# A hybrid decoder block on one core: another form of the routing, the first gather and the last expert block

## The chip, the core and the metric

The kernel runs on one core of one Trainium2 chip. The metric is the time of the program on the device in microseconds (us), the median of three runs: 1419.67 us (1419.36 to 1420.41). Engine names are those of the profile: PE is TensorE, PEld its weight loads, DVE is VectorE, ACT is ScalarE, POOL is GpSimd, SP is SyncE, which issues nearly all loads.

## What is computed

One decoder layer over 256 tokens of width 2048, all in float32. Cut to what matters:

```python
h = rms_norm(x, norm_mix_g);  proj = h @ w_in          # 2048 -> 7168 columns
o = concat([moba_attention(...), hgrn2(...)])          # 8 heads of attention, 8 of gated recurrence
x = x + o @ w_out
h2 = rms_norm(x, norm_ffn_g)
# routing: 4 groups, 4 experts in a group; the best group, then the best two experts in it
grp_w, grp_idx = top_k(softmax(h2 @ w_grp + b_grp), 1)
top_w, top_idx = top_k(softmax(expert logits of that group), 2)
top_w = top_w / sum(top_w) * grp_w
x = x + sum over the 16 experts: ((silu(h2 @ w_gate) * (h2 @ w_up)) * weight) @ w_down
return rms_norm(x, final_norm_g)
```

An expert has three weight matrices of 2048 x 1024 float32, 8 MB each. All 16 experts together are 403 MB, and each is read once.

## The kernel before

**First part** (to about 475 us): the projections, attention and recurrence, then `w_out` in two halves of the contraction (`proj_n`, L366, and the loop after L715). The weights come in 1 MB pieces through two raw halves `shared[8][:, 0]` and `[:, 1]` (`issue_raw`, L103), ACT and DVE split each into a high and a low part (`units`, L305), and PE multiplies. Background work stands in a queue of generators, `bgq`: after each unit `step(k)` (L234) lets it go on by k steps. In the second half of `w_out` the last two column blocks are 256 wide (blocks 3 and 4), and each block appends an `out_block` (L688): DVE adds the block to `X`, ACT takes its square sums into `ssq`, PE transposes it, DVE copies the transposes, PE multiplies them by the router's weights `wr` into `pl`.

**Routing** (L723 to L787): when the queue is empty, `pl` is copied and folded into the logits `plt` (L734 to L738), the root of the mean square is taken, Z is made (L746), and `first_max` (L750) finds the first maximum twice by maximum, comparison, multiplication by a falling count, maximum and comparison. `selb` marks the chosen experts of each token, five small products count ranks (`pr`), and `rk` holds the rank of each token in each expert. `keep_busy` (L729) puts products without use between these steps on PE. `weights_of_routes` (L797) makes the routing weights `comb`, in its last line it writes `cmaxi`, which at the very end decides whether an expert had more than 64 tokens (a branch not taken here).

**Experts** (from L932): each expert has room for 64 tokens (`CAP`). `gather_matrix(e)` makes a 256 x 64 matrix with one entry for each token taken; `gather` (L850) multiplies it with `X` in 512-wide products into one two-bank tile, with a copy by ACT of each bank; `turn` (L863) transposes the result into `xg` and multiplies by the norm's gain. `stream` (L903) runs over the four pieces of the gate (`ga`) and of up (`up`), 16 products of 512 columns for each piece, of which two run side by side in the two halves of the array. Then `hid` = silu(ga) * up, its transposes `hT`, and four pieces of the down matrix into `pd`. `scatter` (L892) adds the result to `acc` in the next expert, behind the first piece of its gate. The order on PE is that of the program (`mmo`, `transpose`); elsewhere a planner orders what is ready. For expert e + 1 the gather stands between `hid` and the down pieces of expert e.

**Loads.** A piece is 2 MB (`pieces`, L247). Twelve loads are issued before the experts (`early_loads`, L249): eight in the course of the first part (`ahead`, L303), the others when the queue is empty (L724). Piece 8 takes the whole of slot 8, that is both raw halves together. Piece 0 is loaded in halves, the second one into a slot that `w_out` uses until its end. Each piece that PE has used up lets `advance` (L822) put the next load on SP's queue, into the slot of an earlier piece: from piece 12 on the nine slots of `ring` in turn, so that piece n waits for the reading of piece n - 9 or n - 10. The loads are in order on SP's queue. In expert 0 the tile `rest`, which holds `hid`, takes the slot of piece 7, the last one of up (L951). `final_gain` (L922), 16 products and four copies, stands behind the third gate piece of expert 1.

**Last expert** (L985 to L1025): the down matrix comes by four column blocks in two halves each. Block b goes into half of one bank of `pd`, a two-bank tile, ACT copies it to `osl`; `spread(b)` (L989) multiplies it into `pz` behind the first half of block b + 1; DVE adds that to `acc`, ACT squares it with a sum into `fs`, POOL multiplies by the final gain (DVE in block 3). At the end the root of the mean square (`rstd`, L198), the scaling of `y` by DVE and ACT in two halves each, and four stores on SP's queue.

Of the kernel before, what the change touches and what calls it, by code (L numbers as in the profile page):

```python
# [19 lines left out]
P = 128  # L20
# [17 lines left out]
def hybrid_block_kernel(  # L38
# [149 lines left out]
    rev = cst.tile([P, 4], F32, name="rev")  # L188
    nc.gpsimd.iota(rev, pattern=[[-1, 4]], base=4, channel_multiplier=0,
                   allow_small_or_imprecise_dtypes=True)  # L190
# [51 lines left out]
    def drain():  # L242
        while bgq:
# [6 lines left out]
                   (8, 8), (9, 9), (10, 7), (0, 1, 1)]  # L250
    ring = [d[1] for d in early_loads if len(d) == 2 and d[0] != 7]
# [17 lines left out]
    def load():  # L269
# [5 lines left out]
        if len(at) == 2:  # L275
            hf, s = at
            wt = single(s, [P, 2048], name="wt")
# [88 lines left out]
    def proj_n(aTh, aTl, c0=0, c1=NC, w=512):  # L366
# [3 lines left out]
        while c < c1:  # L370
            for hi, lo in units():
# [8 lines left out]
                step(2 if c0 else 1)  # L380
# [306 lines left out]

    def out_block(b, col, w, pp, last):  # L688
# [10 lines left out]
        for j in range(0, k, 2):  # L699
            xT = xTs[xi[0] % 2]  # L700
            xi[0] += 1
            pt = psmall().rearrange("p (j t) -> p j t", j=2)
            for i in range(2):
                for n in range(NT):
                    nc.tensor.transpose(
                        pt[:, i, n * P:(n + 1) * P],
                        x2[:, n, bs].rearrange("p (q j) -> p j q", j=k)[:, j + i], ident)
            V.tensor_copy(xT, pt)
            yield
            for i in range(2):  # L710
                mm(pl[32 * i:32 * i + 32], wr[:, col // P + j + i], xT[:, i],
                   start=b == 0 and j == 0, stop=b == 4)
# [16 lines left out]
    def keep_busy(k, ps, lhs, rhs):  # L729
        for i in range(k):  # L730
            mm(ps[0:lhs.shape[1], 0:P], lhs, rhs, start=True, stop=True)

    keep_busy(8, busy, ident, x2[:, 1, D - P:])
    lt = dist1[0:64]  # L734
    V.tensor_copy(lt, pl)
    plt = psmall()[:, :40].rearrange("p (n e) -> p n e", n=NT)
    for n in range(NT):
        mm(plt[:, n], lt[:, n * P:(n + 1) * P], fold[0:64], start=True, stop=True)  # L738


    r2 = small8[:, 2:4]
    V.tensor_reduce(r2, ssq, AX.X, ALU.add)
    rstd(r2, r2, D)
    Z = cst.tile([P, 5, NT, 4], F32, name="Z")
    for n in range(NT):
        V.scalar_tensor_tensor(Z[:, :, n], plt[:, n].rearrange("p (g e) -> p g e", g=5),  # L746
# [3 lines left out]
    def first_max(dst, src, m, tmp, vm, k):  # L750

        V.tensor_reduce(m, src, AX.X, ALU.max)
        V.tensor_tensor(tmp, src, m.unsqueeze(2).to_broadcast([P, k, 4]), ALU.is_equal)
        V.tensor_tensor(tmp, tmp, rev.unsqueeze(1).to_broadcast([P, k, 4]), ALU.mult)
        V.tensor_reduce(vm, tmp, AX.X, ALU.max)
        V.tensor_tensor(dst, tmp, vm.unsqueeze(2).to_broadcast([P, k, 4]), ALU.is_equal)

    Zf = Z.rearrange("p g n e -> p (g n) e")
    ma = cst.tile([P, 10], F32, name="ma")
    mb = cst.tile([P, 8], F32, name="mb")  # L760
    vm = cst.tile([P, 10], F32, name="vm")
    tmp = cst.tile([P, 10, 4], F32, name="tmp")
    M1 = cst.tile([P, 10, 4], F32, name="M1")
    M2 = cst.tile([P, 8, 4], F32, name="M2")
    E2 = cst.tile([P, 8, 4], F32, name="E2")
    keep_busy(8, busy, Z.rearrange("p g n e -> p (g n e)"), ident)
    first_max(M1, Zf, ma, tmp, vm, 10)
    keep_busy(6, busy, M1.rearrange("p a e -> p (a e)"), ident)
    V.scalar_tensor_tensor(E2, M1[:, 0:8], -1e30, Zf[:, 0:8], ALU.mult, ALU.add)
    first_max(M2, E2, mb, tmp[:, 0:8], vm[:, 0:8], 8)  # L770
    V.tensor_tensor(M2, M2, M1[:, 0:8], ALU.add)
    gm = M1[:, 8:10].rearrange("p n g -> p g n").unsqueeze(3).to_broadcast([P, 4, NT, 4])
    selb = cst.tile([P, 4, NT, 4], BF16, name="selb")
    V.tensor_tensor(selb, M2.rearrange("p (g n) e -> p g n e", g=4), gm, ALU.mult)
    pr = psmall()[:, :48].rearrange("p (a g e) -> p a g e", a=3, g=4)
    mm(pr[:, 0], before, selb[:, :, 0], start=True, stop=True)
    mm(pr[:, 1], ones, selb[:, :, 0], start=True, stop=False)
    mm(pr[:, 1], before, selb[:, :, 1], start=False, stop=True)
# [353 lines left out]
```

## Time and profile before

| | us |
|---|---|
| median of 3 runs | 1419.67 |
| the profiled execution | 1415.9 |
| its span, first to last instruction | 1414.1 |
| PE busy | 1322.3 (94%) |
| DVE busy | 432.9 (31%) |
| ACT busy | 275.3 (19%) |
| POOL busy | 17.5 (1%) |
| DMA: mean over the span | 342 GB/s, 483.75 MB |

The profile shows one execution. A row of the timeline has start, duration, engine, line, operation, out<-in, and in brackets the idle time of the engine before it with what ended that. Rows of the same operation behind one another are merged (x8). A float32 product of PE has two records, a transpose one. "To landing" is the time from a load's issue to its arrival. Nearly all of the DMA's bytes are expert weights, so its share of busy time tells by stage whether the weights flow without a break.

### The profile page before, as it was taken

The numbers are of one execution on the slowest core, as the hardware profiler recorded it, in microseconds if no ns is written. First come the engines' busy times: TensorE is split into PE (matmuls) and PEld (weight loads), VectorE is DVE, ScalarE is ACT, GpSimd is POOL, SyncE is SP. The second block draws the span as 40 slices with busy tenths as digits, with TensorE's granted clock in tenths as the row PEclk, the third lists the DMA queues.
The fourth block names the chain that finished last, engine by engine and source line by source line (L and its number), as shares of the span: only waits on it lengthen the run. The fifth ranks groups of instructions, "written<-read, shape, count | busy, mean of one in ns | idle before, by whom it ended". The sixth has DMA issues, their size and how long they took to land.

```text
span 1414.1 us, 16501 instructions
## 1 busy us (share of the span) xinstructions
PE 1322.3 (94%) x7091; PEld 721.7 (51%) x7091; DVE 432.9 (31%) x647; ACT 275.3 (19%) x409; POOL 17.5 (1%) x47
## 2 busy tenths in 40 slices
PE   9999999999999999999999999889898998989885
PEld 8999998998887633333333323223232232322323
DVE  5555567567555411121121112111121111211012
ACT  5553542542543201000000000000000000000002
POOL 2000000000000000000000000000000000000002
PEclk9999999999999999999999999999999999999998
DMA  6655553455687599999999999999999999999995
GB/s 237 241 163 173 179 173 126 157 183 185 222 338 286 219 409 378 427 428 428 427 428 427 429 427 427 428 429 428 426 430 427 428 427 427 428 427 429 427 410 197
DMA packets 85726, 483.75 MB, mean 342 GB/s; under 512 B 16849, under 2 KB 19601, under 8 KB 60817
## 3 DMA queue, kind: packets, MB, share of 16 engines
q1 hardware_dynamic: 85520, 482.62, 84.6%
q8 instruction: 57, 0.93, 0.3%
q14 instruction: 21, 0.16, 0.0%
q10 hardware_dynamic: 128, 0.03, 0.0%
HBM read 480.54 MB, written 2.10 MB: 341 GB/s over the span
## 4 chain that ended last, share of the span: by engine, by line
PE 66%; DMA 29%; DVE 2%; ACT 2%; issue 1%; ACTq 0%; SPq 0%; DVEq 0%
DMA wt<-in_w_up_dram 25%; PE pd L831 12%; PE pp L340 12%; PE up L831 8%; PE ga L831 6%; PE pp L376 5%; PE pp L377 5%; PE pp L378 5%; PE pn L831 4%; DMA wt<-in_w_gate_dram 3%; PE pt L834 2%; PE pw L482 1%; PE psc L831 1%; DVE rest L967 1%; ACT xn L860 1%
## 5 line engine op out<-in xcount | busy, mean ns | idle before, releaser
L831 PE MATMUL up<-wt,xg 128*64 128x512 f32 x1024 | 231.2, 597 | 38.4 <-DMA wt<-in_w_up_dram 38.4
L831 PE MATMUL ga<-wt,xg 128*64 128x512 f32 x1024 | 226.8, 595 | 4.2 <-DMA wt<-in_w_gate_dram 4.2
L831 PE MATMUL pd<-wt,rest 128*64 128x512 f32 (+1 forms) x1088 | 224.7, 569 | 2.8 <-ACT rest L1016 2.0
L321 DVE TENSOR_TENSOR whl<-sh,whl 128x1024 fp32r<-128x1024 f32 (+1 forms) x145 | 175.5, 1216 | 121.9 <-ACT whl L319 116.8
L319 ACT ACTIVATE whl<-sh 128x1024 fp32r<-128x1024 f32 (+1 forms) x145 | 151.7, 1051 | 223.4 <-PE pp L378 106.0
L340 PE MATMUL pp<-hTh,whl 128*128 128x256 f32 x1024 | 190.4, 285 | 0.0
L831 PEld LDWEIGHTS up<-wt,xg 128*64 128x64 f32 x1024 | 69.4, 137 | 188.1 <-issue 120.3
L340 PEld LDWEIGHTS pp<-hTh,whl 128*128 128x128 f32 x1024 | 161.3, 192 | 0.2
L831 PEld LDWEIGHTS ga<-wt,xg 128*64 128x64 f32 x1024 | 72.9, 137 | 153.7 <-issue 149.8
L831 PEld LDWEIGHTS pd<-wt,rest 128*64 128x64 f32 x1088 | 76.2, 137 | 139.2 <-issue 128.9
L340 PE MATMUL pp<-hTl,whl 128*128 128x256 f32 x512 | 145.2, 284 | 1.1 <-DVE hTl L394 1.0
L901 DVE TENSOR_TENSOR rest<-rest,psc 128x1024 f32<-128x1024 f32 x28 | 34.2, 1221 | 254.4 <-PE psc L831 253.0
L340 PEld LDWEIGHTS pp<-hTl,whl 128*128 128x128 f32 x512 | 98.2, 192 | 1.9 <-DVE hTl L394 1.7
L887 DVE COPY pT<-pt 128x256 f32<-128x256 f32 x16 | 6.8, 424 | 292.5 <-PE pt L834 292.5
L376 PE MATMUL pp<-whl,hTh 128*128 128x512 f32 x192 | 77.5, 404 | 0.0
L860 ACT ACTIVATE xn<-pn 128x512 f32<-128x512 f32 x32 | 19.1, 597 | 295.6 <-PE pn L831 295.6
L378 PE MATMUL pp<-whl,hTl 128*128 128x512 f32 x192 | 75.3, 392 | 0.0
L377 PE MATMUL pp<-whl,hTh 128*128 128x512 f32 x192 | 74.9, 390 | 0.0
L831 PE MATMUL pn<-X,pg 128*64 128x512 f32 x256 | 61.2, 599 | 13.1 <-ACT xn L860 12.4
L831 PE MATMUL psc<-rest,pT 64*128 64x512 f32 x240 | 63.7, 628 | 7.0 <-DVE rest L901 7.0
L957 ACT ACTIVATE rest<-ga 128x512 f32<-128x512 f32 x16 | 9.6, 597 | 281.3 <-PE ga L831 253.6
L981 ACT ACTIVATE rest<-pd 128x1024 f32<-128x1024 f32 x15 | 15.4, 1025 | 234.3 <-PE pd L831 234.3
(273 smaller groups left out, 977.6 us busy)
## 6 DMA issues: line engine op xcount, KB each, us to landing
wt<-in_w_gate_dram SPq DMA_DIRECT2D x63, 2048.0 KB, 39.1
wt<-in_w_up_dram SPq DMA_DIRECT2D x60, 2048.0 KB, 34.9
wt<-in_w_down_dram SPq DMA_DIRECT2D x59, 2048.0 KB, 36.9
sh<-in_w_in_dram SPq DMA_DIRECT2D x55, 1024.0 KB, 5.1
sh<-in_w_out_dram SPq DMA_DIRECT2D x16, 1024.0 KB, 5.7
wt<-in_w_down_dram SPq DMA_DIRECT2D x8, 1024.0 KB, 14.7
wt<-in_w_up_dram SPq DMA_DIRECT2D x8, 1024.0 KB, 28.8
wt<-in_w_gate_dram SPq DMA_DIRECT2D x2, 1024.0 KB, 10.8
```

The source lines that it names most:

```text
L319: S.activation(t[:, 0, a:b], rw, AF.Copy)
L321: V.tensor_tensor(t[:, 1, a:b], rw, t[:, 0, a:b].bitcast(F32), ALU.subtract)
L340: r = mm(*a, **kw)
L376: mm(pp[:, n], ah, hi[:, k], start=c == c0, stop=False)
L377: mm(pp[:, n], ah, lo[:, k], start=False, stop=False)
L378: mm(pp[:, n], al, hi[:, k], start=False, stop=c == c1 - 1)
L482: mm(pa[:, 2 * h + n], k[:, h, ts], q[:, h, ts].rearrange("p (b z m) -> p b z m", z=2, m=m)[:, :, 1], start=True, stop=True)
L831: tc.keep_in_program_order(mm(*a, **k))
L834: tc.keep_in_program_order(nc.tensor.transpose(dst, src, ident))
L860: S.activation(xn[:, j], ps[:, j], AF.Copy)
L901: V.tensor_tensor(acc[n][:, bs], x2[:, n, bs] if e == 0 else acc[n][:, bs], ps.rearrange("p z f -> p (z f)"), ALU.add)
L981: S.activation(osb, pd, AF.Copy)
```

## The change

- **Loads.** Piece 8 is loaded in two halves of 1 MB straight into the raw halves of slot 8, each as soon as its own half is free.
- **Router products.** In the 256-wide blocks `step(4)` instead of `step(2)`. Block 3 ends the accumulation in `pl`, then copies it and folds it into `plt` at once, and takes the square sums of blocks 0 to 3 together. Block 4 is transposed by token halves, and its products go straight into `plt` with the transposes as the stationary side.
- **Choice of experts by counting.** Instead of two `first_max`, two comparisons of all pairs (160 elements), a choice between them by the mask `tri`, and a sum give each expert's rank; rank 0 is the best group, rank under 2 the two experts. `cmax` is taken from a copy that ACT makes, behind the gather matrix. `keep_busy` has 3, 6 and 3 products instead of 8, 8 and 6, and is kept in program order.
- **First gather.** For expert 0 `gather_turned` multiplies 128 x 128 blocks of `X`, taken as the stationary side, with the gather matrix (64 columns), so that the result is already turned; a quarter is 8 products and one multiply by the gain. One and a half quarters come before the first gate piece, the others behind its pieces 0 and 1. `weights_of_routes` is issued behind the first quarter's multiply. The gather for expert 1 stands behind the down pieces of expert 0. In all later experts `gather` uses two one-bank tiles.
- **`final_gain`** moves from expert 1 to expert 6.
- **Last expert.** The blocks go into one-bank tiles `ga` and `up` in turn. `acc` of the last 512 columns is put into PSUM by four products with the identity ahead of the transposes of `hid`, and `spread(3)` adds to it there; squares and the last scaling read PSUM (ACT the lower 256 columns, DVE the upper ones with a sum). The stores go out on SP's and ACT's queues.

```diff
-                   (8, 8), (9, 9), (10, 7), (0, 1, 1)]
+                   (8, 0, "raw"), (8, 1, "raw"), (9, 9), (10, 7), (0, 1, 1)]
...
+            wt = shared[8][:, hf] if s == "raw" else single(s, [P, 2048], name="wt")
...
-                step(2 if c0 else 1)
+                step(4 if w == 256 else 2 if c0 else 1)
...
+            if b == 4:
+                for n in range(NT):
+                    pn = psmall()[:, 0:2 * P].rearrange("p (j t) -> p j t", j=2)
+                    for i in range(2):
+                        transpose(pn[:, i], xj[:, n, j + i])
+                    V.tensor_copy(xT[:, :, n * P:(n + 1) * P], pn)
+                for n in range(NT):
+                    for i in range(2):
+                        mmo(plt[0][:, n], xT[:, i, n * P:(n + 1) * P],
+                            wr[:, col // P + j + i, 0:20], start=False, stop=i == 1,
+                            skip_group_check=True)
+                return
...
+        if b == 3:
+            V.tensor_reduce(sq4, ssq[:, :, 0:4], AX.X, ALU.add)
+            V.tensor_scalar(sq4, sq4, EPS * D, None, ALU.add)
+            lt = dist1[0:64]
+            V.tensor_copy(lt, pl)
+            plt[0] = psmall()[:, :40].rearrange("p (n e) -> p n e", n=NT)
+            for n in range(NT):
+                mm(plt[0][:, n], lt[:, n * P:(n + 1) * P], fold[0:64], start=n == 0, stop=False,
+                   skip_group_check=True)
...
-    keep_busy(8, busy, ident, x2[:, 1, D - P:])
+    keep_busy(3, busy, ident, ident)
...
-    first_max(M1, Zf, ma, tmp, vm, 10)
...
-    first_max(M2, E2, mb, tmp[:, 0:8], vm[:, 0:8], 8)
+    V.tensor_tensor(wins, zo, zs, ALU.is_gt)
+    V.tensor_tensor(ties, zo, zs, ALU.is_ge)
+    V.copy_predicated(wins, tri.unsqueeze(1).to_broadcast([P, 10, 4, 4]), ties)
+    V.tensor_reduce(rank, wins, AX.X, ALU.add)
+    V.tensor_scalar(G1n, rank[:, 8:10], 0.0, None, ALU.is_equal)
...
+    V.scalar_tensor_tensor(selb.rearrange("p g n e -> p (g n) e"), rank[:, 0:8], 2.0,
+                           G1.unsqueeze(2).to_broadcast([P, 8, 4]), ALU.is_lt, ALU.mult)
...
+    def gather_turned(xg, pg, b, q0, q1, pt):
+        xb = x2[:, :, b * 512:(b + 1) * 512].rearrange("t n (p q) -> t n q p", q=4)
+        for q in range(q0, q1):
+            for n in range(NT):
+                mmo(pt[:, q], xb[:, n, q], pg[:, n], start=n == 0, stop=n == 1)
+        if q1 == 4:
+            xg_made.append(V.tensor_tensor(
+                xg[:, 4 * b:4 * b + 4], pt,
+                gfe[:, 4 * b:4 * b + 4].unsqueeze(2).to_broadcast([P, 4, CAP]), ALU.mult).ins)
...
-    xg = turn(gather(gather_matrix(0)))
-    weights_of_routes()
+    pg = gather_matrix(0)
+    cmax_of_ranks()
...
+    gather_turned(xg, pg, 0, 0, 4, pturn())
+    pt1 = pturn()
+    gather_turned(xg, pg, 1, 0, 2, pt1)
...
+            if e == 0 and i == 0:
+                gather_turned(xg, pg, 1, 2, 4, pt1)
+                gather_turned(xg, pg, 2, 0, 4, pturn())
+                with tc.issue_after(xg_made[0]):
+                    weights_of_routes()
+            if e == 0 and i == 1:
+                gather_turned(xg, pg, 3, 0, 4, pturn())
...
-            if i == 2 and e == 1:
+            if i == 2 and e == 6:
                 gf = final_gain()
...
+        if e == NE - 1:
+            part0 = pscr().rearrange("p (n f) -> p n f", n=NT)
+            part = [[part0[:, 0], part0[:, 1]], [pscr()[:, 0:256], ptwo("part")[:, 0, 0:256]]]
+            for n in range(NT):
+                for z in range(2):
+                    lo = 1536 + z * 256
+                    mmo(part[z][n], ident, acc[n][:, lo:lo + 256], start=z == 1 or n == 0,
+                        stop=False, skip_group_check=True)
-        if e + 1 < NE:
+        if 0 < e < NE - 1:
             xn = gather(pg)
...
+        if e == 0:
+            xg = turn(gather(pg))
...
+        po = pq.tile([P, 512], F32, name="up" if b % 2 else "ga")[:, 0:256]
...
-        S.activation(osl[:, b], pd[:, b % 2, 0:256], AF.Copy)
+        S.activation(osl[:, b], po, AF.Copy)
...
+    for n in range(NT):
+        S.activation(jk[:, 0:256], part[0][n], AF.Square, accum_out=fs[:, n, 3:4])
+    for n in range(NT):
+        V.tensor_copy(high[0][n], part[1][n])
+        V.scalar_tensor_tensor(high[1][n], part[1][n], 1.0, high[0][n], ALU.mult, ALU.mult,
+                               accum_out=rs[:, n:n + 1])
...
+    for n in range(NT):
+        for z, half in enumerate((low, high)):
+            V.scalar_tensor_tensor(half[1][n], part[z][n], rf[:, n:n + 1],
+                                   gf[:, 1536 + 256 * z:1792 + 256 * z], ALU.mult, ALU.mult)
+        (nc.sync, S)[n].dma_start(out=out_v[:, n, 1024:], in_=y[n][:, 1024:])
```

## Rows read from the trace of the kernel before

**Rows 1.** Stretches: us, busy us (records) by engine, granted clock, DMA share, GB/s.

```profile
446.00:500.00 54.00, 51.98 (x319) 36.23 (x319) 23.69 (x68) 15.27 (x28) 0.00 (x0) 1.00 0.62 238
...
580.00:800.00 220.00, 213.19 (x986) 73.71 (x984) 38.53 (x67) 11.86 (x17) 0.00 (x0) 1.00 1.01 428
800.00:1393.00 593.00, 531.93 (x2452) 179.39 (x2448) 89.28 (x144) 31.92 (x51) 3.86 (x4) 1.00 1.00 424
```

**Rows 2.** Chain of waits of the whole span: start, us, what.

```profile
487.29 1.94 PE pn L831 x8
...
518.81 1.74 PE pn L831 x8
...
525.51 13.88 PE pd L831 x64
...
554.48 3.82 PE pt L831 x32
...
806.72 34.37 DMA wt<-in_w_up_dram
```

**Rows 3.** L285, the one load of SP issued at 551.09.

```profile
DMA to landing us min/median/max: 7.2/7.2/7.2
```

**Rows 4.** L285, the one load of SP issued at 561.92.

```profile
DMA to landing us min/median/max: 8.1/8.1/8.1
```

**Rows 5.** Timeline of the end, from 1376 us, all engines.

```profile
1376.42 0.75 PE L834 MATMUL pt<-ident,rest 128*128 128x128 f32 x4 [0.86 <-DVE rest L961]
...
1382.17 1.95 PE L831 MATMUL pd<-wt,rest 128*64 128x256 f32 x16 [0.54 <-ACT rest L1016]
...
1396.34 1.95 PE L831 MATMUL pd<-wt,rest 128*64 128x256 f32 x16
...
1399.04 1.13 PE L831 MATMUL pz<-rest,pT 64*128 64x256 f32 x8 [0.75 <-ACT rest L1016]
...
1401.54 0.19 ACT L1002 ACTIVATION_READ_ACCUMULATOR jk<-rest 128x1 f32 x1
...
1403.52 1.42 DVE L1022 TENSOR_SCALAR y<-y,small 128x1024 f32<-128x1024 f32 x2 [0.34 <-ACT small L201]
...
1404.30 2.90 SPq L1025 DMA_DIRECT2D out_dram<-y  x4
```

**Rows 6.** Timeline of the routing, 474 to 491 us, PE and DVE.

```profile
474.44 1.63 PE L705 MATMUL pw<-ident,X 128*128 128x128 f32 x8
...
477.98 1.38 PE L731 MATMUL pp<-X,ident 128*128 128x128 f32 x10
...
479.29 0.62 PE L738 MATMUL pw<-fold,dist 64*128 64x20 f32 x4
480.02 0.38 DVE L746 SCALAR_TENSOR_TENSOR Z<-pw,small,bias 128x20 f32<-128x20 f32 x2 [1.50 <-PE pw L738]
480.44 0.20 DVE L752 TENSOR_REDUCE ma<-Z 128x10 f32<-128x40 f32 x1
...
483.16 0.19 DVE L774 TENSOR_TENSOR selb<-M,M 128x32 bf16<-128x32 f32 x1
...
484.62 1.94 PE L831 MATMUL pn<-X,pg 128*64 128x512 f32 x8 [0.70 <-PE pw L780]
...
490.61 3.65 PE L831 MATMUL ga<-wt,xg 128*64 128x512 f32 x16
```

**Rows 7.** Groups by line and form on DVE, 100 to 500 us: busy us, mean ns.

```profile
L691 DVE TENSOR_TENSOR X<-X,pp 128x256 f32<-128x256 f32 x4 | 1.5, 416 | 6.8 <-PE pp L378 6.8
```

**Rows 8.** L278, the one load of SP issued at 475.01.

```profile
DMA to landing us min/median/max: 12.1/12.1/12.1
```

**Rows 9.** Timeline of expert 0 between up and down.

```profile
518.86 0.60 ACT L957 ACTIVATE rest<-ga 128x512 f32<-128x512 f32 x1 [27.69 <-PE up L831]
```

**Rows 10.** Stretches of the end, columns as in rows 1.

```profile
1393.00:1400.00 7.00, 5.85 (x48) 3.50 (x48) 1.29 (x2) 2.06 (x7) 3.66 (x3) 1.00 0.04 13
1400.00:1405.00 5.00, 0.17 (x2) 0.00 (x0) 4.31 (x9) 3.06 (x7) 0.00 (x0) 0.80 0.03 7
```

More of the change, by code (lines that the diff above doesn't have):

```diff
@@ L730, in keep_busy @@
         for i in range(k):
-            mm(ps[0:lhs.shape[1], 0:P], lhs, rhs, start=True, stop=True)
-    keep_busy(8, busy, ident, x2[:, 1, D - P:])
[L734 to L738, printed above, removed]
+            mmo(ps[0:lhs.shape[1], 0:P], lhs, rhs, start=True, stop=True)
+    keep_busy(3, busy, ident, ident)
     r2 = small8[:, 2:4]
-    V.tensor_reduce(r2, ssq, AX.X, ALU.add)
@@ L768, in hybrid_block_kernel @@
-    keep_busy(6, busy, M1.rearrange("p a e -> p (a e)"), ident)
-    V.scalar_tensor_tensor(E2, M1[:, 0:8], -1e30, Zf[:, 0:8], ALU.mult, ALU.add)
-    first_max(M2, E2, mb, tmp[:, 0:8], vm[:, 0:8], 8)
-    V.tensor_tensor(M2, M2, M1[:, 0:8], ALU.add)
-    gm = M1[:, 8:10].rearrange("p n g -> p g n").unsqueeze(3).to_broadcast([P, 4, NT, 4])
+    G1 = cst.tile([P, 8], F32, name="G1")
+    G1n = G1.rearrange("p (g n) -> p n g", n=NT)
+    keep_busy(6, busy, Z.rearrange("p g n e -> p (g n e)"), ident)
@@ L777, in hybrid_block_kernel @@
-    mm(pr[:, 1], ones, selb[:, :, 0], start=True, stop=False)
-    mm(pr[:, 1], before, selb[:, :, 1], start=False, stop=True)
-    mm(pr[:, 2], ones, selb[:, :, 0], start=True, stop=False)
-    mm(pr[:, 2], ones, selb[:, :, 1], start=False, stop=True)
+    mmo(pr[:, 0], before, selb[:, :, 0], start=True, stop=True)
+    mmo(pr[:, 1], ones, selb[:, :, 0], start=True, stop=False)
+    mmo(pr[:, 1], before, selb[:, :, 1], start=False, stop=True)
+    mmo(pr[:, 2], ones, selb[:, :, 0], start=True, stop=False)
@@ L781, in hybrid_block_kernel @@
+    mmo(pr[:, 2], ones, selb[:, :, 1], start=False, stop=True)
+    keep_busy(3, busy, ident, ident)
     rk = cst.tile([P, NT, 4, 4], F32, name="rk")
@@ L795, in hybrid_block_kernel, with cmax_of_ranks @@
     cmaxi = cst.tile([1, 1], I32, name="cmaxi")
+    def cmax_of_ranks():
+        with tc.issue_after(pg_last[0]):
+            V.tensor_reduce(cmax, prc, AX.X, ALU.max)
+            V.tensor_copy(cmaxi, cmax[:1])
     def weights_of_routes():
+        V.tensor_reduce(ma, Zf, AX.X, ALU.max)
+        V.tensor_scalar(M2, rank[:, 0:8], 2.0, None, ALU.is_lt)
         V.tensor_tensor(Zf, Zf, ma.unsqueeze(2).to_broadcast([P, 10, 4]), ALU.subtract)
@@ L987, in hybrid_block_kernel, with halves @@
     y = [yt[:, n] for n in range(NT)]
+    def halves(t, b):
+        return t[:, b * 512:(b + 1) * 512].rearrange("p (z f) -> p z f", z=2)
     def spread(b):
         bs = slice(b * 512, (b + 1) * 512)
+        if b == 3:
+            for n in range(NT):
+                for z in range(2):
+                    mmo(part[z][n], pT[64 * z:64 * z + 64, n], osl[64 * z:64 * z + 64, b],
+                        start=False, stop=z == 1 or n == 1, skip_group_check=True)
+            return
         pz = ptwo("pz")
@@ L996, in spread @@
         for n in range(NT):
[L997 to L998 removed]
+            V.tensor_tensor(halves(acc[n], b), halves(acc[n], b),
                             pz[:, :, n * 256:(n + 1) * 256], ALU.add)
```

114 lines of the change are left out of this document (64 added, 50 removed).

## The prediction

> **What bounds the kernel now.** Read the stretches first [rows 1]. From 800 to 1393 us the DMA engines are busy the whole time at 424 GB/s: the expert weights set the pace and TensorE waits for them. From 580 to 800 both are full, TensorE 213 of 220 us and the DMA at 428 GB/s. From 446 to 500, around the routing, the DMA is at 0.62 of its time. So once the stream of weights flows without a break, the end is the number of bytes still to come, and a front edit pays only in so far as the last break before 580 ends earlier. The chain of waits [rows 2] says who makes the breaks: TensorE's own work, entry after entry, from the routing to expert 5; the first wait for weights is at 806.72. Each load on SP's queue reuses a slot of nine, and goes out when TensorE has read the slot's last weights. The last two loads that come late go out at 551.09 (behind the second gate piece of expert 1) and 561.92 (behind the fourth, after `final_gain`); they need 7.2 and 8.1 us to land [rows 3, 4], at 558.3 and 570.0. A steady 2 MB takes 2.097 MB / 428 GB/s = 4.9 us, and from 570.0 on the stream has no break. The end after the last weights is a third stage with its own limit: TensorE, ScalarE and VectorE in turn [rows 5].
>
> So there are two sums: the time at which the load of 551.09 goes out and what lands behind it, and the tail.
>
> **Front: routing.** TensorE ends w_out at 474.44 and starts the gather at 484.62 [rows 6]: 10.2 us.
> - Block 3's transposes, router products and the fold now lie ahead of w_out's end, where TensorE is full. Four transposes are half of the eight of 474.44 at most, some 0.5; the fold took 0.62 [rows 6]; the router products, four records too, some 0.5. That is 1.6, less a run-out here and there: +1.5 (0 if it finds gaps, +2.0 with pipeline changes).
> - What is left after w_out's end is block 4. VectorE adds two 256-wide tiles (0.42 each by [rows 7], the second overlapping), each half is transposed, copied (taken as another 0.42) and multiplied straight into the logits' PSUM tile: add 0.2 after w_out, first transposes at 0.7, copies to 2.0, products and their run-out to 2.7, logits Z at 2.8. Before, Z started 5.6 after w_out (480.02). The sum of squares needs one add, one reciprocal and one root behind ScalarE's squares, some 2.6, so the logits don't wait for it.
> - Z to `selb` took 480.02 to 483.16, of which 0.42 is Z itself and 2.7 are thirteen instructions of about 0.21 (the first at 480.44) [rows 6]. Now there are four over 160 elements and one small one. Between 0.20 for 40 elements and 0.42 for 256 [rows 6, 7] 160 lie at 0.32; with 0.02 of spacing 4 x 0.34 + 0.2 = 1.6.
> - `selb` to gather stays 1.46 (483.16 to 484.62), or 0.1 less without the reduction for `cmax`.
> Sum: 2.8 + 0.42 + 1.6 + 1.4 = 6.2. Against 10.2 that is -4.0, with +1.5 from block 3.
>
> **Front: the transposed gather.** Before, gather and turn took 484.62 to 490.61, 6.0 us. Now 32 products of a 128-column stationary block of X with 64 moving columns stand there; a product is two records on TensorE (two fold products are four records). Ten records with a 128-column stationary side took 1.38, four took 0.62 [rows 6]: six more cost 0.76, 0.127 each. 64 x 0.125 = 8.0, +2.0, in four parts. The first 24 records (3.0) come before the first expert product, the other 40 (5.0) between the gate pieces, behind which SP's next slots are freed. The gain of the early start is therefore spent by the end of expert 0's gate. VectorE's part is off the path: its 0.4 multiply per quarter runs beside eight further records. `weights_of_routes` moves behind the first multiply: fifteen instructions of 0.2 and one ScalarE exponential, some 4 us on VectorE's queue; queued behind it is the multiply of quarter 1, which TensorE needs about 6 us after the first. So nothing, with 1 us if it slips.
>
> The first gate piece's second half is loaded at 475.01 and landed 12.1 later, at 487.1 [rows 8]. The new start is 474.44 + 1.5 + 6.2 + 3.0 = 485.1, and the half is needed 1.74 later (four steps of 0.43; eight took 3.65 with their run-out [rows 6]), at 486.9. The split load of piece 8 lets its first half start while the second raw half is still read, but the loads behind wait for w_out's last products, which are later by the 1.5. I take +0.4 (0 to 0.8).
>
> **Front: expert 0's down block.** Now expert 1's gather comes behind the down block. Before, up ended at 518.81 and the down block began at 525.51: 6.7 with the gather in it [rows 2]. In expert 0 the silu starts only after up has ended (518.86, its target takes the slot of up's last piece) [rows 9]. So TensorE is bare for silu 0.6, multiply 0.7, transposes 0.7, copy 0.7 and the hand-overs: 3.0. The gather afterwards, in two tiles without the wait between its halves, costs 6.0 less that wait, which is 487.29 - 484.62 - 1.74 = 0.9 [rows 2, 6]: 5.1. So 8.1 against 6.7: +1.4. Slots of down pieces come free 3 to 4 us earlier, but that lead is lost again at the next late load.
>
> **Sum of the front.** -4.0 + 1.5 + 2.0 + 0.4 + 1.4 = +1.3: the load of 551.09 goes out at 552.4. `final_gain` (3.82 [rows 2]) leaves expert 1 for expert 6, where TensorE waits for weights anyway; its cover is those waits (34 us at 806.72), and without it would cost 3.8. So the third load behind no longer waits: three loads land in a row: 552.4 + 7.2 + 2 x 4.9 = 569.4, or, with 8.1 for a load that starts the stream anew, 570.3, against 570.0. I take the later one, since this load finds the engines idle. Front: **+0.4** (rounded up), between -1.5 and +2.
>
> **Tail.** In the last expert each of three blocks waits 0.54 to 0.75 for ScalarE's copy out of the shared tile (the first at 1382.17) [rows 5]. With one-bank tiles these three, 2.0 in all, go. Four products that put acc into PSUM come in ahead of the transposes of 1376.42: sixteen records run two at a time in 1.95, so a step is 0.24, and eight records with 128 columns have no partner: 1.9, of which 0.86 was idle: +1.0. A half block takes 1.95 and a spread 1.13, each 0.07 less to the next one's start; block 0 ended at 1382.17 - 0.54 = 1381.63. Then 1381.6 + 1.0 + 2 x (1.88 + 1.06 + 1.88) + 2.94 = 1395.2 for the last half block instead of 1396.34: **-1.1**. The weights are there: from 1393 to 1400 the DMA moves 13 GB/s [rows 10].
> From the spread (1399.04) to the scaling (1403.52) it took 4.48. Now VectorE reads the first finished bank after 0.7, four 256-wide instructions of 0.4, then two adds, a reciprocal and the root 1.0: 3.3, ScalarE's two squares (2 x 0.8) beside it: **-1.2**. On ScalarE a sum that goes along is a second instruction of 0.19 [rows 5]. The Trainium skill (VectorE: DVE Perf Modes, "Two Vector instructions with no wait between them") says that of VectorE too: its two sums would then cost 0.4, and the tail would gain 0.4 less; no trace here shows one.
> Output: scaling to first store 0.78 as before (1404.30); the later ones come over two queues, the last one after 0.75 + 0.4 + 4 x 0.4 = 2.75 instead of about 3.0, and the four stores still share the same engines: 0. Tail: **-2.2**, between -1.0 and -3.0.
>
> Total: +0.4 - 2.2 = **-1.8**. The profiled execution took 1415.9 (span 1414.1), 3.8 under the median of 1419.67; I carry the difference over: 1417.9.
>
> **Rivals.** *A, the front gains too:* block 3's products fill gaps ahead of w_out's end and the half piece comes in time. 1.9 less, the load goes out at 550.5 and its followers at their quickest, front -1.5, tail -2.7: 1415.5. For it: `step(4)` puts the work one unit earlier. Against: TensorE shows no gaps there.
> *B, slower:* the turned gather's weight loads don't overlap. Eight transposes with X stationary took 1.63, 0.20 a record [rows 6], though partly waiting. 64 x 0.20 = 12.8 instead of 8.0, on TensorE's path up to the load of 551.09: +4.8, so 1422.7. It turns the sign from 0.153 a record on. Against it: 0.127 in the ten-record row.
> *C, the clock falls:* expert 0 leaves TensorE bare for 3 us with 0.7 of transposes within. After its end at 1400.2 the granted clock is 0.80 on average up to 1405 [rows 10], so it fell from 2.4 to 1.2 GHz inside. If it fell here, the down block (13.9) would take between 0 and 13.9 more; no row shows how long it would last, and I take 4, since work follows at once: 1421.9. Against it: the idle stretch is broken by the transposes. The Trainium skill (TensorE: Matmul & The Clock Gate, "What's actually happening") holds idle time to be what throttles the array; by that rule this change is risky here and in the routing, where three products remain of eight to keep it busy.
> *D, the tail doesn't do what it says:* the copies out of PSUM and the products with acc take the place of the waits; tail -0.6, front +0.4: 1419.5.
>
> **How the numbers follow.** Forecast 0.46 (1416.3 to 1419.5), A 0.28, B 0.08, C 0.05, D 0.13. A measurement of this kernel can tell about 0.2%, 2.8 us, from no change. Faster by that: most of A and a seventh of the forecast, 0.33; slower: B and half of C, 0.11; the rest, 0.56, is the same. The range takes in A and D with the bounds of the front, 1414.5 to 1421.5.
>
> **What would show it.** Gather starts some 2.5 us earlier than 484.62; expert 0's gate ends within 1 us of 504.5 (490.61 and 32 steps of 0.43); the load behind expert 1's second gate piece goes out at 551 to 553 and the stream is unbroken some 18 us later; `final_gain` stands at a wait for weights; the last half block starts near 1395.2 and the scaling 6 us later, both counted from the last weights. I am wrong if the turned gather costs over 10 us, if expert 1's gate starts before 539 or after 542, or if the last weights move by more than 2 us.

## The result, and the profile after

The changed kernel takes 1429.88 us (median of 6 runs, 1428.39 to 1430.8) against 1419.57 for the kernel before: ratio 1.0079, 95% interval 1.0069 to 1.0090. It is slower by 10 us; the forecast was 1417.9. The profiled execution of the changed kernel took 1430.8, span 1429.1; it was the slowest of its six, and that of the kernel before was one of its shortest (1415.9), so the two profiles lie further apart than the medians.

The chain of waits of the changed kernel around expert 0 (start, us, what). `pt L694 x24` and `x16` ahead of 511 are the 64 records of the turned gather, `pt x16` at 553.73 is expert 1's gather.

```profile
485.44 5.83 PE pt L694 x24
491.27 5.42 PE ga L694 x16
496.69 5.79 PE pt L694 x24
502.49 4.93 PE ga L694 x16
507.42 3.88 PE pt L694 x16
...
532.65 1.28 ACT L1019
...
536.89 16.84 PE pd L694 x64
553.73 3.43 PE pt L694 x16
...
558.61 1.43 PE ga L694 x5
```

Read it against [rows 2, 6]. The gather takes 5.83 + 5.79 + 3.88 = 15.5 us on TensorE, where gather and turn took 6.0. Two gate pieces of 16 records take 5.42 and 4.93, where 16 such records take 3.43 at the full clock (553.73 is as many of the same width). A table load of ScalarE, 1.28, stands between up and the silu. The down block takes 16.84 instead of 13.88. Expert 1's gate starts at 558.61; the prediction called itself wrong after 542.

Stretches of the changed kernel (columns as in rows 1; behind the last bracket stands the granted clock, 1.00 is 2.4 GHz and 0.50 is 1.2 GHz):

```profile
17.10:20.50 3.40, 3.40 (x18) 3.40 (x18) 1.71 (x2) 1.47 (x3) 0.00 (x0) 0.50 0.16 52
...
488.10:494.90 6.80, 6.80 (x24) 4.22 (x25) 2.83 (x19) 0.24 (x1) 0.00 (x0) 0.50 0.08 34
494.90:501.80 6.90, 6.90 (x30) 5.47 (x29) 0.42 (x1) 0.00 (x0) 0.00 (x0) 0.99 0.80 302
501.80:505.20 3.40, 3.40 (x11) 1.43 (x13) 0.42 (x1) 0.00 (x0) 0.00 (x0) 0.50 0.02 7
...
535.90:542.70 6.80, 6.02 (x16) 1.72 (x16) 0.69 (x1) 0.00 (x0) 0.00 (x0) 0.50 0.76 323
...
500.00:580.00 80.00, 75.99 (x327) 29.19 (x328) 10.35 (x19) 4.70 (x6) 0.00 (x0) 0.94 0.78 313
```

The clock was at half in three stretches around expert 0, and in two of them TensorE was busy for the whole stretch (6.80 of 6.80, 3.40 of 3.40). From 500 to 580 the DMA runs at 313 GB/s, where the kernel before has 400 (its row is below), and after 580 at 428 as in [rows 1]: the lost time lies in front of 580. The stretch at 17 us, far ahead of the change, makes everything behind it 2.8 us later in this execution; the differences to the kernel before below leave these 2.8 out.

```profile
500.00:580.00 80.00, 77.63 (x374) 28.35 (x370) 10.59 (x19) 6.40 (x10) 0.00 (x0) 1.00 0.96 400
```

The load behind expert 1's second gate piece, issued at 570.46; in the kernel before it went out at 551.09 [rows 3]:

```profile
DMA to landing us min/median/max: 8.5/8.5/8.5
```

It goes out 19.4 - 2.8 = 16.6 us later, and the weights behind it land without a break.

The end of the changed kernel, timeline of all engines [rows 5]:

```profile
1405.52 1.95 PE L694 MATMUL ga<-wt,rest 128*64 128x256 f32 x16 [0.22 <-DMA wt<-in_w_down_dram]
...
1413.13 1.95 PE L694 MATMUL up<-wt,rest 128*64 128x256 f32 x16
...
1415.83 0.91 PE L694 MATMUL pt<-rest,pT 64*128 64x256 f32 x5 [0.75 <-ACT rest L1099]
...
1417.39 0.08 DVE L1111 DVE_READ_ACCUMULATOR y<-pt,rest 128x1 f32 x1
...
1418.19 0.08 DVE L1111 DVE_READ_ACCUMULATOR y<-part,acc 128x1 f32 x1
...
1419.27 0.75 DVE L1118 TENSOR_SCALAR y<-y,small 128x1024 f32<-128x1024 f32 x1 [0.34 <-ACT small L1116]
```

The waits for ScalarE's copy between the half blocks are gone. One half block now waits for weights (0.22). From the spread to the scaling it takes 1419.27 - 1415.83 = 3.44 instead of 4.48. From the landing of the last weights to the end of the span it is 15.8 us instead of 19.3. These two are the far ends: over all the profiles of this case it is 18.3 to 19.3 with the old tail (four kernels) and 15.8 to 17.1 with the new one (ten), 18.7 and 16.5 in the mean, a difference of 2.2.

### The profile page after: what moved, and what is told of

Read it like the earlier page. It is cut to its first block, busy times and chain, and to the rows that moved or that the text cites. A ratio compares the mean times of both kernels' runs of the same rounds, so it can differ in the third digit from the quotient of the medians.

```text
span 1429.1 us, 16577 instructions
## 1 busy us (share of the span) xinstructions
PE 1345.4 (94%) x7123; PEld 741.6 (52%) x7123; DVE 436.5 (31%) x654; ACT 273.6 (19%) x408; POOL 18.0 (1%) x49
## 3 DMA queue, kind: packets, MB, share of 16 engines
q10 hardware_dynamic: 416, 1.08, 0.2%
## 4 chain that ended last, share of the span: by engine, by line
PE 62%; DMA 34%; DVE 2%; ACT 1%; issue 0%; SPq 0%; ACTq 0%; DVEq 0%
DMA wt<-in_w_up_dram 16%; PE pp L344 12%; DMA wt<-in_w_down_dram 9%; DMA wt<-in_w_gate_dram 8%; PE ga L694 8%; PE pd L694 8%; PE up L694 7%; PE pp L380 5%; PE pp L381 5%; PE pp L382 5%; PE pt L694 4%; PE psc L694 2%; PE pt L697 2%; PE pw L486 1%; DMA sh<-in_w_in_dram 1%; DVE rest L947 1%
## 5 line engine op out<-in xcount | busy, mean ns | idle before, releaser
L694 PE MATMUL up<-wt,xg 128*64 128x512 f32 x1024 | 231.1, 597 | 37.6 <-DMA wt<-in_w_up_dram 37.5
L694 PE MATMUL ga<-wt,xg 128*64 128x512 f32 x1024 | 232.5, 606 | 12.6 <-DMA wt<-in_w_gate_dram 12.6
L694 PE MATMUL pd<-wt,rest 128*64 128x512 f32 x944 | 206.8, 595 | 2.1 <-DMA wt<-in_w_down_dram 2.1
L694 PEld LDWEIGHTS up<-wt,xg 128*64 128x64 f32 x1024 | 69.3, 137 | 187.3 <-issue 120.1
L694 PEld LDWEIGHTS ga<-wt,xg 128*64 128x64 f32 x1024 | 74.0, 139 | 164.6 <-issue 160.8
L694 PEld LDWEIGHTS pd<-wt,rest 128*64 128x64 f32 x944 | 65.6, 137 | 132.6 <-issue 120.8
L895 ACT ACTIVATE xn<-pt 128x512 f32<-128x512 f32 x30 | 17.9, 597 | 274.0 <-PE pt L694 274.0
L694 PE MATMUL psc<-rest,pT 64*128 64x512 f32 x240 | 63.7, 628 | 7.0 <-DVE rest L947 7.0
L694 PE MATMUL pt<-X,pg 128*64 128x512 f32 x240 | 54.0, 592 | 0.0
## 6 DMA issues: line engine op xcount, KB each, us to landing
wt<-in_w_down_dram SPq DMA_DIRECT2D x8, 1024.0 KB, 15.8
```

The costliest lines, as they stand in the source:

```text
L694: tc.keep_in_program_order(mm(*a, **k))
L895: S.activation(xn[:, j], ps, AF.Copy)
```

## The experiments

Times are medians in us; the kernel before took 1418.3 to 1418.5 beside the first eleven, 1417.15 beside the last, 1419.57 beside the changed kernel. Its single times spread from 1415.3 to 1420.4, and its median moved with them, so a difference between two variants taken at different times holds to 1 or 2 us. The theory at the start: the turned gather's records take twice the price put on them, and the clock falls beside them and in the bare stretch of expert 0. The rivals: the clock falls because the routing keeps TensorE less busy; or the records are slow for another reason than their stride.

**Expert 0's gather back in one piece.**

```diff
-    gather_turned(xg, pg, 0, 0, 4, pturn())
...
+    xg = turn(gather(pg))
+    weights_of_routes()
```

> The changed kernel, with expert 0's gather and turn back in one piece ahead of the stream, as before the change. Theory 1 (the turned gather's 64 records at 0.24 us, and the clock that falls beside them): the gather goes from 15.5 to 6.0 us, and the two gate pieces at half clock (5.42 and 4.93 us) return to 3.43, so 13 us of the front come back: 1429.9 - 13 = about 1417, and the granted clock stays at 1 between 485 and 510. Theory 2 (the records are slow, but the clock falls because the routing has 3 products for 8 to keep TensorE busy): a stretch at half clock stays right behind the routing, only 9.5 come back: about 1420.4.

1413.19, ratio to before 0.9963 (0.9950 to 0.9977): 16.7 less than the changed kernel, and faster than the kernel before. Theory 1 holds and is rather too small: gather and turn take 5.0 here (483.92 to 488.95), not the 6.0 of the kernel before, and the table load is off the path. There is a half clock inside the routing, none behind it up to 520.8, so the shorter keep-busy groups are not what slows the gate. In expert 0's bare stretch the clock falls here too; the timeline of TensorE and the two stretches:

```profile
520.10 5.35 PE L694 MATMUL pd<-sh,rest 128*64 128x512 f32 x16 [0.78 <-DVE rest L1026]
```

```profile
479.90:483.30 3.40, 3.40 (x20) 2.82 (x20) 2.17 (x13) 0.67 (x3) 0.00 (x0) 0.50 0.96 405
...
520.80:524.20 3.40, 3.40 (x10) 0.98 (x8) 0.00 (x0) 0.00 (x0) 0.00 (x0) 0.50 0.98 419
```

The first 16 records of the down block take 5.35 (3.65 at the full clock, below). From up's end at 517.1 to the down block it is 3.0 us, exactly the prediction's sum, since here the silu's table is loaded early (at 488.23).

**Expert 1's gather back between up and down.**

```diff
-        if 0 < e < NE - 1:
+        if e < NE - 1:
             xn = gather(pg)
...
-        if e == 0:
-            xg = turn(gather(pg))
```

> The changed kernel, with expert 1's gather back between expert 0's up and down products; the turned gather of expert 0 stays. Theory 1 (the bare stretch for silu and transposes lets the clock fall): up's end to the gate of expert 1 goes from 4.3 + 16.84 + 4.9 = 26.0 us to 6.7 + 13.9 = 20.6, no half clock between 530 and 545: 1429.9 - 5.5 = about 1424.4. Theory 2 (the clock falls whatever stands there, as an after-effect of the turned gather): the down block stays at 16.8, only 2.5 come back: about 1427.4.

1424.05: 5.8 less than the changed kernel (5.0 by the ratios to the kernel before, 1.0079 and 1.0044), as theory 1 has it. The first two falls beside the turned gather stay, the third is gone:

```profile
486.60:493.40 6.80, 6.80 (x24) 4.22 (x26) 2.84 (x19) 0.24 (x1) 0.00 (x0) 0.50 0.02 7
500.20:503.60 3.40, 3.40 (x12) 1.44 (x13) 0.42 (x1) 0.00 (x0) 0.00 (x0) 0.50 0.06 27
503.60:540.00 36.40, 36.37 (x170) 15.32 (x168) 5.23 (x14) 2.97 (x4) 0.00 (x0) 1.00 0.85 347
```

They begin 2.6 us behind the start of the first part (484.01) and 5.1 behind that of the second (495.14); in the changed kernel these were 2.7 and 5.1 (in the run with the table early, below, 5.3, 4.7 and 4.5 behind the starts of the three parts). TensorE had issued the turned gather's records without a gap.

**Both gathers back.** The two edits above together.

> The changed kernel with both gathers as before the change; the routing by counting, the split load of piece 8, the later final gain and the new tail stay. If the two parts add up, 1429.9 - 13 - 5.5 = about 1411.5. By the single steps, against the kernel before: routing -2.5 (-4.0, and +1.5 for block 3's products ahead of it), final gain 0 to -1.7, tail -3.5, so 1419.6 - 6 to 1419.6 - 7.7 = 1412 to 1413.5. Rival: the shorter keep-busy groups of the routing let the clock fall behind it, as in the changed kernel; then 3 to 4 us more, 1415 to 1417.

1409.35, ratio 0.9939 (0.9924 to 0.9954): the best version here, 9 us under the kernel before. The half clock is absent from 483 to 580 in its profile. The rest of the change is thus a gain, of more than the single steps gave.

**The pace of the records by themselves.**

```diff
+            if i == 1 and e == 3:
+                pb = pscr()
+                for s, k in ((4, 64), (1, 64), (2, 64), (8, 64), (4, 16), (4, 128)):
+                    xs = x2[:, 0, 0:128 * s].rearrange("t (p q) -> t q p", q=s)[:, 0]
+                    for r in range(16):
+                        mmo(pb[:, 0:k], xs, ident[:, 0:k], start=True, stop=True)
```

> The kernel before, with six groups of 16 float32 products (two records each) set between two gate pieces of expert 3; their results go nowhere. Stationary side: 128 rows of X, 128 columns at a stride of 4, 1, 2, 8 (64 moving columns), then stride 4 with 16 and with 128 moving columns. Theory 1 (the strided columns of the stationary side set the pace): 0.233 us a record at stride 4, about 0.11 at stride 1, and stride 4 keeps 0.233 with 16 moving columns. Theory 2 (the weight load and the 64 moving columns don't overlap, as the prediction's rival had it): 0.23 at every stride with 64 columns, and about 0.17 with 16.

It could not tell them apart, because the clock fell 4.5 us into it and stayed down:

```profile
664.10:668.70 4.60, 4.60 (x22) 4.54 (x20) 0.00 (x0) 0.00 (x0) 0.00 (x0) 1.00 1.01 431
668.70:706.20 37.50, 37.50 (x167) 37.50 (x167) 0.00 (x0) 0.00 (x0) 0.00 (x0) 0.50 0.28 118
```

TensorE was never idle in these 37.5 us. Stride 4 kept 0.233 a record on both sides of the fall; stride 1 took 0.213 at the half clock. So the pace at stride 4 doesn't follow the clock.

The same in short groups, one in each of the experts 2 to 7 (`st, k = ((4, 64), (1, 64), (2, 64), (8, 64), (4, 16), (1, 16))[e - 2]`, six products each):

> The kernel before, with six products (twelve records) set between two gate pieces of each of the experts 2 to 7, short so that the clock stays up; their results go nowhere. Stationary columns of X at a stride of 4, 1, 2, 8 with 64 moving columns, then 4 and 1 with 16. Theory 1 (the distance of the stationary columns sets the pace): 0.233 us at strides 4 and 8 whatever the moving side, about 0.11 at strides 1 and 2 at the full clock (they took 0.213 at the half clock). Theory 2 (float32 products with X take 0.21 to 0.235 always): 0.21 or more at every stride.

Timeline of TensorE, twelve records to a line, the moving side being the last number:

```profile
609.09 3.01 PE L831 MATMUL pt<-ident,X 128*128 128x64 f32 x12
...
665.54 1.55 PE L831 MATMUL pt<-ident,X 128*128 128x64 f32 x12
...
720.52 1.63 PE L831 MATMUL pt<-ident,X 128*128 128x64 f32 x12
...
775.58 3.06 PE L831 MATMUL pt<-ident,X 128*128 128x64 f32 x12
...
833.76 2.97 PE L831 MATMUL pt<-ident,X 128*128 128x16 f32 x12
...
891.82 1.51 PE L831 MATMUL pt<-ident,X 128*128 128x16 f32 x12
```

At the full clock, from one start to the next: 0.233 at stride 4, 0.111 at 1, 0.118 at 2, 0.238 at 8, and with 16 moving columns 0.233 and 0.111 again. The distance of the stationary columns sets the pace of these products, 16 or 64 columns moving: 16 and 32 bytes apart cost twice what 4 and 8 do. Right behind two of the three slow groups (at 778.6 and at 836.6) the clock fell to half; behind the fast groups it did not. The Trainium skill (SBUF — State Buffer, "Door 1: The DMA port swizzle (why `[64,N]` ≈ `[32,N]`)") has a rule that bears on it: SBUF is read in lines of 16 bytes, and full bandwidth wants two hits in a line. By that rule strides 1 and 2 are fast and 4 and 8 slow, as measured. Its next sentence says of the free stride "4 fp32"; if that means a step of four elements, the measurement is against it. The transposes, also at stride 4, take 0.12 a record (last section), so the rule as measured here holds for products and not for them.

**The turned gather with neighbouring columns, expert 1's gather back.** The rows of expert 0's gate and up weights are loaded in the order that goes with it.

```diff
-        xb = x2[:, :, b * 512:(b + 1) * 512].rearrange("t n (p q) -> t n q p", q=4)
+        xb = x2[:, :, b * 512:(b + 1) * 512].rearrange("t n (q p) -> t n q p", q=4)
...
-                gfe[:, 4 * b:4 * b + 4]
+                gffn[:, 4 * b:4 * b + 4]
```

> As the run with expert 1's gather back (1424.05 us), but the turned gather of expert 0 takes 128 neighbouring columns of X as its stationary side instead of every fourth; the rows of expert 0's gate and up weights are loaded in the matching order. Theory 1 (every fourth column, 16 bytes apart, sets the pace of 0.233 us a record): about 0.12 a record, the 64 records fall from 15.5 to 8 us: 1424 - 7.5 = 1416.5, and 1413 if the clock stays up as well. Theory 2 (a float32 product with 128 rows of X takes 0.23 whatever the stride): within 1 us of 1424.

1412.73: 11.3 less than with every fourth column, theory 1 with the clock. TensorE:

```profile
483.40 2.86 PE L697 MATMUL pt<-pg,X 128*128 128x64 f32 x24
...
488.80 1.94 PE L697 MATMUL ga<-wt,xg 128*64 128x512 f32 x8 [0.67 <-DMA wt<-in_w_gate_dram]
490.67 2.89 PE L697 MATMUL pt<-pg,X 128*128 128x64 f32 x24
...
497.07 2.00 PE L697 MATMUL pt<-pg,X 128*128 128x64 f32 x16
```

2.86 + 2.89 + 2.00 = 7.75 for 64 records, where the prediction had 8.0. The clock is full from 483 to 545:

```profile
483.00:500.00 17.00, 16.22 (x105) 9.93 (x105) 5.09 (x28) 1.61 (x3) 0.00 (x0) 1.00 0.67 243
500.00:545.00 45.00, 44.96 (x212) 15.66 (x208) 4.96 (x12) 3.99 (x5) 0.00 (x0) 1.00 0.97 401
```

And the wait for the first piece's second half, which the prediction put at 0.4 (0 to 0.8), is there: 0.67 (1.08 in the next run). Even so this is 3.4 slower than the plain gather (1409.35).

**The same edit in the changed kernel, and nothing else.**

> The changed kernel as it is, with expert 1's gather behind the down block, but with neighbouring columns of X in the turned gather (and the rows of expert 0's gate and up weights to match). This gives the prediction's price for a record, 0.125 us, to the whole change. If that was the prediction's only large error, it takes what the prediction said: 1417.9, or 1416.5 by the sums from the run with the gather back (1412.7, +2.5 for the order, +1.3 for the table load of the silu). If the bare stretch of expert 0 lets the clock fall as well, 3 more: 1418.5 to 1419.5, with a half clock beside the down block.

1418.99, ratio 1.0007 (0.9998 to 1.0016): the third answer, 10.9 less than the changed kernel. It is 1.1 over the forecast of 1417.9; but that stood 1.8 under the kernel before, and this run stands 0.7 over it (1418.32 beside it). The turned gather is as in the run before; the down block is slowed for 3.4 us:

```profile
524.80:528.20 3.40, 3.40 (x10) 0.98 (x8) 0.00 (x0) 0.00 (x0) 0.00 (x0) 0.51 1.03 439
```

**The silu's table loaded early, in the changed kernel.**

```diff
                 with tc.issue_after(xg_made[0]):
                     weights_of_routes()
+                S.activation(vm[:, 0:2], Zf[:, 8, 0:2], AF.Silu)
```

> The changed kernel with one small silu on ScalarE behind the routing weights, so that the table for expert 0's silu is loaded there and not after up's end. Theory 1 (the table load stands on the path): up's end to the down block 4.3 to 3.0 us, 1429.9 - 1.3 = 1428.6. Theory 2 (the longer bare stretch is also what lets the clock fall): the down block goes from 16.8 back to 13.9 as well, 1425.6. Rival: TensorE's wait is only moved, 1429.9.

1426.07: 3.8 less, or 3.3 by the ratios to the kernel before (1.0079 and 1.0056): between the two theories, nearer to theory 2. The first 16 records of the down block in the changed kernel, and the silu and these records here:

```profile
536.89 6.54 PE L694 MATMUL pd<-sh,rest 128*64 128x512 f32 x16 [0.78 <-DVE rest L1039]
```

```profile
533.58 0.60 ACT L1020 ACTIVATE rest<-ga 128x512 f32<-128x512 f32 x1 [41.75 <-PE up L694]
...
536.48 3.65 PE L694 MATMUL pd<-sh,rest 128*64 128x512 f32 x16 [0.78 <-DVE rest L1040]
```

The silu starts with up's end, and these records take 3.65 instead of 6.54. 1.3 is the table load; the fall beside the down block, worth 3.0, is missing in this profile. In its place there is a third one beside the gate (at 490.6, 500.8 and 511.1; the changed kernel has two there), which makes the gate's last two pieces 8.78 long instead of 7.09. That the early table keeps the clock up in the bare stretch is thus not shown by this run alone.

**The bare stretch filled,** in the kernel with the first gather back.

```diff
+        if e == 0:
+            pk = pscr()
+            for r in range(10):
+                mmo(pk[:, 0:P], ident, ident, start=True, stop=True)
```

> The run with the first gather back (1413.2 us), with ten float32 products of the identity set in expert 0's bare stretch between up and the transposes, on TensorE alone and ahead of what waits for the silu. Theory 1 (idle time lets the clock fall): the half clock of 520.8 to 524.2 is gone, 1.7 us less, 1411.5. Theory 2 (what comes before it, or the execution, decides): the half clock stays or the time stays at 1413.2; the products themselves take 2.2 us of a stretch that is 1.4 us idle before the transposes, so up to 0.8 more, 1414.

1412.73 against 1413.19, ranges 1411.49 to 1414.08 and 1410.61 to 1414.02: the times can't be told apart. In the profile the fall is gone:

```profile
522.36 3.65 PE L694 MATMUL pd<-sh,rest 128*64 128x512 f32 x16 [0.78 <-DVE rest L1030]
```

Inconclusive: the run before this one had a bare stretch of 3.0 us as well and no fall, without any filling. All profiles of this case together say more: four have the bare stretch (the changed kernel, neighbouring columns in it, the first gather back, the table early) and the clock fell in three of them; of the ten others, where the gather or the filling stands there, it fell in none.

**The tail alone,** on the kernel before: its last expert's blocks, `spread`, sums and stores replaced by the new ones.

> The kernel before with the new last expert and end alone: three one-bank tiles, acc's last quarter added in PSUM, VectorE and ScalarE sharing the sums, output over two queues. If the tail is worth what the changed kernel's traces show from the last weights to the end, 19.25 to 15.8 us: -3.5; by the prediction -2.2; if it only trades waits for copies -0.6.

1417.01, ratio 0.9988 (0.9979 to 0.9997): -1.3, between the forecast (-2.2) and rival D (-0.6), and its interval, -3.0 to -0.4, holds both. Its trace has 16.8 us from the last weights to the end, 2.4 less than before. The means of all profiles (18.7 and 16.5) speak for the forecast.

**The final gain early again,** in the kernel with both gathers back.

```diff
-            if i == 2 and e == 6:
+            if i == 2 and e == 1:
                 gf = final_gain()
```

> As the run with both gathers back (1409.35 us), with the final gain again in expert 1 instead of expert 6. By the landings: the loads behind expert 1's second and third gate pieces keep their times, the one behind the fourth goes out 3.8 us later, at 558.7, and lands at 566.5 to 567 instead of 566.2: +0.3 to +0.8, which can hardly be told from no change. If instead its 3.8 us on TensorE count in full: 1413.2.

1413.86, 4.5 slower (3.8 by the ratios 0.9966 and 0.9939): the rival. The load behind expert 1's fourth gate piece [rows 4] goes out at 562.92, not at 558.7. The gain's products on the timeline, the stretch behind their start, and that load's way:

```profile
552.11 5.00 PE L694 MATMUL pt<-frow,ident 16*128 16x128 f32 x32
```

```profile
554.60:561.50 6.90, 6.90 (x25) 3.59 (x25) 0.00 (x0) 1.39 (x3) 0.00 (x0) 0.51 0.81 347
```

```profile
DMA to landing us min/median/max: 7.9/7.9/7.9
```

It lands at 570.8, 4.6 later than with the gain in expert 6 (566.2). In this execution the clock was at half from 554.6, beside the gain and the gate piece behind it. The profiles of the tail alone and of the first record test have such a fall at this place too, those of the kernel before and of the short record test don't. How much of the 4.5 is the clock is open: the single times run from 1411.12, with the highest mean clock of the six (0.996), to 1414.93.

**The final gain late, on the kernel before.** The reverse of that edit, alone.

> The kernel before with one line changed: the final gain moves from expert 1 to expert 6. Theory 1 (its products on TensorE hold back the load behind expert 1's fourth gate piece, and in most executions the clock falls beside them): the same 4.5 us as between the runs with both gathers back, 1418.3 - 4.5 = 1413.8, and the spread of the single times becomes smaller. Theory 2 (the prediction's price: the third load merely follows the second without a break): 1.0 to 1.5 us, 1417.

1415.61 against 1417.15, ratio 0.9990 (0.9981 to 0.9999): 1.5, theory 2. The single times spread as before (1413.71 to 1418.24). So the gain's place is worth 1.5 on the kernel before and 4.5 in the one with the faster front. By the landings the third load is the last break left there; that this and not the clock makes the difference is argued and not shown.

## Why the prediction was wrong, point by point

**The step that failed** is the price of a turned gather's record. The prediction took 0.125 us from the ten records of 477.98 [rows 6], whose stationary columns are neighbours, for products that take every fourth column. They cost 0.233 a record, 0.242 with the starts of the parts: 15.5 instead of 8.0, over the bound of 10 that the prediction gave itself. Rival B had the right place and part of the size (0.20 from the transposes of 474.44: +4.8, measured +7.5), but for another reason, that weight loads and products don't overlap: with 16 moving columns or 64 the pace is the same. It was given 0.08.

**Its second cost was not in the sum at all.** While these records run, the clock falls, and the gate pieces behind them take 2.0 and 1.5 more. Rival C named the routing as well, but priced a fall in the bare stretch alone, at 4 us, and gave it 0.05. The fall there came too: the down block took 3.0 more. The price of the gather's clock and records is shown for both together by the neighbouring columns (-11.3 in time, both gone). The clock's part in the bare stretch is shown by expert 1's gather back in its place and by the count over all profiles (three falls in four, none in ten). How often it falls there is open: with 3.0 us bare it fell in one profile and not in another. The table load of 1.28 between up and the silu was a term that the prediction did not have.

**The sum with the measured terms.** Gather +7.5, gate pieces +3.5, down block +3.0, table load +1.3, block 3's products +0.4 (w_out ended 1.9 later, forecast 1.5), the half piece -0.4 (it landed at 490.94, ahead of the gate's first record at 491.20), expert 1's gather -0.2 (4.9, forecast 5.1): 15.1 on top of the forecast +1.3 is 16.4, and the load behind expert 1's second gate piece went out 16.6 later. The third load behind landed 18.7 - 2.8 = 15.9 later, and the tail gave 3.5 back in this execution: 12.4, where the two profiled executions are 1430.8 - 1415.9 - 2.8 = 12.1 apart. The medians are 10.3 apart.

**What held.** The routing: from w_out's end to the gather 6.3 us, forecast 6.2. But that is so in four of the nine profiles with the new routing (6.4 from the start of w_out's last record); in the other five the clock is at half inside it, as in the run with the first gather back, and it takes 7.7 to 7.8. In the five profiles with the old routing, which has more products without use, it never is (10.3). So the saving was 3.9 us or 2.6; that it is the fewer products that let the clock fall was not tested by itself. Timeline of the changed kernel:

```profile
479.35 0.75 DVE L705 TENSOR_TENSOR X<-X,pp 128x256 f32<-128x256 f32 x2 [2.41 <-PE pp L382]
...
482.02 0.38 DVE L778 SCALAR_TENSOR_TENSOR Z<-pw,small,bias 128x20 f32<-128x20 f32 x2 [0.57 <-PE pw L694]
482.44 0.32 DVE L796 TENSOR_TENSOR dist<-Z 128x160 f32<-128x160 f32 x1
...
484.03 0.19 DVE L803 SCALAR_TENSOR_TENSOR selb<-rank,G 128x32 bf16<-128x32 f32 x1
```

Logits 2.9 us behind w_out's end at 479.1 (2.8), 0.32 for 160 elements (0.32), `selb` 2.0 behind the logits' start (1.6 + 0.42). The tail's mechanism: spread to scaling 3.44 (3.3), no wait for ScalarE between the half blocks, and 2.2 by the means of all profiles (2.2). VectorE's sums did come as a second instruction, as the Trainium skill says (VectorE: DVE Perf Modes, "Two Vector instructions with no wait between them"), but of 0.08 us each, not ScalarE's 0.19 [rows 5]; the 0.4 kept for it was not needed.

**What was mis-sized.** The final gain's move was worth 1 to 1.5 in the sum. On the kernel before that is right (1.5); behind a faster front it is 4.5, with the clock in it. The runs with the tail alone and with the final gain early differ by the routing, the split load and the gather in two one-bank tiles together: 1413.86 - 1417.01 = -3.2. The routing was forecast at -4.0 + 1.5 = -2.5, and the two tiles save 0.9 to 1.0 for each of the two gathers (5.0 instead of 6.0, and 5.75 instead of 6.7 from up to the down block), so nothing in it is better than forecast; the profile of the second run has the half clock in its routing. Expert 1's gather behind the down block costs 5.8 in the changed kernel, 6.3 behind the gather of neighbouring columns (1418.99 - 1412.73) and 3.8 behind the plain one (1413.19 - 1409.35), forecast 1.4. Of that 1.4, 0.9 to 1.0 was credited to the two tiles, which the version with the gather in its old place has too, so some 2.4 was to be expected; table load (1.3) and clock (1.7 to 3.0) come on top. So of the change's parts the routing, the two tiles, the tail and the final gain's place are worth 9 us together; the two moved gathers cost 20.5 (19.9 by the ratios).

## What to carry to other kernels

Price a matmul by a row with the same layout of the stationary side: the shape alone did not tell a stride of 16 bytes, which here doubled a float32 product's time. A part can fail inside a change whose other parts gain; build the parts alone, and look at the granted clock in the rows before calling a stretch hidden. A gain measured on a kernel with several late loads (1.5 here) need not be its worth once the others are early (4.5).

## What the runs showed of the hardware that was not expected

- A float32 product with 128 stationary columns takes 0.111 us a record at strides of 1 element, 0.118 at 2, 0.233 at 4 and 0.238 at 8, at 2.4 GHz. At 1.2 GHz stride 1 takes 0.213 and stride 4 still 0.233. The transposes of `hid` and of the gathered rows at stride 4 didn't show it: 0.12 from start to start (523.38 to 524.11 in the kernel before).
- The granted clock fell from 2.4 to 1.2 GHz while TensorE issued such records without an idle gap (37.5 of 37.5 us busy in one run, over strides of 4, 1, 2 and 8). The Trainium skill (TensorE: Matmul & The Clock Gate, "What's actually happening") puts it down to how busy TensorE has lately been; by the busy column of the rows, in which the ends of products are modelled, it was busy.
- A table load of ScalarE can stand behind the wait of the instruction that needs it (1.28 us at 532.65) or ahead of it (489.89 in the kernel before, hidden); which one depended on what ScalarE had done before.
